# Gates loaded into the tiles of their results, two additions made by transfers, and sums of squares in two chains taken half a product later, in a hybrid short-convolution and Conformer block

## The chip, the cores and the metric

The kernel runs on one core of a Trainium2 chip, in one launch. The metric is the time on the device in microseconds (us) of one execution; the median of three runs is compared. The names of the engines are those of the profile: PE (TensorE, matmuls), DVE (VectorE), ACT (ScalarE), POOL (GpSimd) and SP (SyncE, which only starts transfers here). Each engine works through its own instructions in a fixed order and waits at an instruction whose inputs, or whose place to write, are not ready.

## The reference

One layer on 1024 rows of 1024 channels in f32: two mixers side by side, merged by sigmoid gates, and a feed-forward layer with SwiGLU behind them.

```python
h = rms_norm(x, norm_mix_g[l]) * (1.0 + sc1) + sh1
proj = jnp.einsum('bsd,de->bse', h, w_in[l])
b_s, c_s, v_s, v_c, gl_c, gate_br = jnp.split(proj, SPLITS[:-1], axis=-1)
y_a = b_s * causal_dwconv(c_s * v_s, conv_short_w[l])
y_a = jnp.einsum('bsc,cd->bsd', y_a, w_short_out[l])
u = v_c * jax.nn.sigmoid(gl_c)
u = causal_dwconv(u, conv_conf_w[l]) + conv_conf_b[l]
u = jax.nn.silu(layer_norm(u, conf_ln_g[l], conf_ln_b[l]))
y_b = jnp.einsum('bsc,cd->bsd', u, w_conf_out[l])
g_a, g_b = jnp.split(jax.nn.sigmoid(gate_br), 2, axis=-1)
mix = jnp.einsum('bsd,de->bse', g_a * y_a + g_b * y_b, w_o[l])
x = x + g1 * mix
h2 = rms_norm(x, norm_ffn_g[l]) * (1.0 + sc2) + sh2
a, bgate = jnp.split(jnp.einsum('bsd,df->bsf', h2, w_ffn_in[l]), 2, axis=-1)
x = x + g2 * jnp.einsum('bsf,fd->bsd', jax.nn.silu(a) * bgate, w_ffn_out[l])
return rms_norm(x, final_norm_g)
```

`sh1, sc1, g1, sh2, sc2, g2` are six vectors of 1024, `silu(c) @ w_ada + b_ada`.

## The kernel before

The activations are held transposed: a tile has 128 channels on its partitions, and the 1024 rows are two halves of 512, called h. Eight tiles j = 0..7 make up a tensor.

Every large product is cut into 2x2 blocks in Strassen-Winograd's way: seven products m ("1" to "7") in place of eight, for each of the two outputs (d = 0, 1, the two groups of four output tiles, which share their sums of operands). Each operand is carried as a high and a low part in fp32r, and three matmuls stand for one: weights' high by high (L553), high by low (L554), low by high (L556). One call of `product` does one (d, m): for p = 0 and 1 four such triples into one PSUM bank, so 24 matmuls, and hands each finished bank to an `evac` function. An argument `between` of `product` is called between p = 0 and p = 1.

The weights of a product come in by a transfer that SP starts (`raw`). Where a sum of blocks is wanted, POOL adds other blocks to it by transfers that accumulate (L368, L403). ACT casts the high part (`wh`, L254, 128x1024), DVE subtracts for the low part (`wl`, L255), two products ahead of their use. The same pair of engines splits the activations (`q4h` and `q4l`, `z2h` and `z2l`, `h20h` and `h20l` and so on).

A scheduler fixes each engine's order when the kernel is built, from costs and from the sizes of the pools of buffers; two pools matter here. `g_tile` gives one of 6 buffers of 128x512, for short-lived tiles: gates (`ga`, `gb`), squares (`sq`), residual inputs (`xr`), reciprocal roots. `s_tile` and `hl_tile` draw on a pool of 58 buffers, for results that live longer (`ma`, and the split operands). A tile's load can start only when the last reader of the buffer's former tile is done.

The stages that the change touches stand in this order:

- **The short branch's output product** (560 to 645 us of the profile). `ya_evac` takes the banks; `out` multiplies a finished block by its gate `ga` into the result `ma[j, h]` (L914 or L918). `gates_a`, called ahead of each product, starts the two loads of gates that the product's results will want: on ACT's queue for m = "2" and on SP's otherwise. Beside it DVE normalizes the other branch (`cv`, `mu`, squares `sq`, sums `suml` for the matmuls `var` at L733), and multiplies the modulation's weights (`ada`, L534).
- **The Conformer branch's output product** (645 to 745 us). `yb_evac` multiplies by the gates `gb` and adds the result to `ma`: either by DVE (L1463) or by a transfer of POOL's that accumulates (L1467). Which one is set by d, row and h. The operands `z1` to `z7` are split meanwhile.
- **The merged product** (745 to 795 us, `mix`, in the order "1267453" of m). `mix_evac` adds the bank to the residual tile `x1[j]`; `x1_done` stores the finished half, squares it on ACT and adds the square to `sums[h]`. For h = 0 DVE adds; for h = 1 the odd j are added by POOL's transfers through `onto` (L618) and the even ones by DVE (L1546). `norm_2_first` splits `sums[0]` into `sumh` and `suml` (L726, L727), sums them over the partitions by two matmuls (L733) and makes the reciprocal root `r2r`. `norm_2_rows` then scales half 0 of the rows k that it is given and splits them (`h2k`, L1622, L1628). `NORM_2_AT` and `NORM_2_ROWS` say at which products of d and m this happens.
- **The feed-forward input products** (from 795 us on), whose first product reads `h20` to `h23`; the sum of half 1 over the partitions is two matmuls (`ss`, L739) in the middle of the product (1, "1"), and its root is taken at L629 to L631.

Of the kernel before, what the change touches and what calls it, by code (L numbers as in the profile page):

```python
# [38 lines left out]
ALU = mybir.AluOpType  # L39
# [5 lines left out]
KC = D // P  # L45
# [44 lines left out]


NORM_2_AT = (1, "5")
NORM_2_ROWS = {(1, "5"): (0, 1, 2, 3), (0, "3"): (4, 5), (1, "3"): (6, 7)}

# [53 lines left out]
def block_kernel(ctx: ExitStack, tc: tile.TileContext, x0, xT, c, vecs, ada, w_first, w_plain, w_duals,  # L150
                 w_short, w_conf, w_o, w_fi, w_fo0, w_fo1, outT):
    nc = tc.nc
# [33 lines left out]
    def hl_tile(name, dt=F32R):  # L186
        return tp.tile([P, H], dt, tag="t", name=name)

    def s_tile(name, dt=F32):
        return hl_tile(name, dt)  # L190

    def g_tile(name):
        return gsp.tile([P, H], F32, tag="gs", name=name)
# [4 lines left out]
    halves = (slice(0, H), slice(H, T))  # L198
# [366 lines left out]
    def product(banks, m, t, evac=None, between=None, y_tile=ps2_tile, z_tile=ps_tile, onto="", by_k=False):  # L565


        w = next_w()
        b = {"1": "x", "6": "x", "7": "x", "4": "x", "2": "y", "5": "z", "3": "z"}[m]
        n = len(t)  # L570
        if by_k:
            for k in range(n):
                for p in range(2):
                    c0 = (p * n + k) * P
                    mm3([banks[b, p]], slice(c0, c0 + P), w, [t[k]], m not in onto and k == 0, k == n - 1, m in onto)
            for p in range(2):
                evac(p, m, banks[b, p])
            return
        for p in range(2):
            if (b, p) not in banks:  # L580
                banks[b, p] = {"x": ps_tile, "y": y_tile, "z": z_tile}[b](b)
            ps = banks[b, p]
            for k in range(n):
                c0 = (p * n + k) * P
                mm3([ps], slice(c0, c0 + P), w, [t[k]], m in "125" and m not in onto and k == 0, k == n - 1, m in "6734" + onto)
            if evac:
                evac(p, m, ps)
            if between and p == 0:
                between()
# [26 lines left out]
    def onto(a, b):  # L616

        return nc.gpsimd.dma_start(a, b, accum_op=ALU.add).ins  # L618
# [125 lines left out]
    gate_dram = {(b, j): dram.tile([P, T], F32, name=f"gate_{b}{j}") for b in "ab" for j in range(KC)}  # L744
# [637 lines left out]
    ma = {}  # L1382

    def ya_evac(d, banks):

        st = {}

        def out(i, row, h, op, ps):
            j = 4 * d + 2 * i + row
            ma[j, h] = s_tile(f"ma{j}{h}")  # L1390
            op(ma[j, h], ps, gas.pop((j, h)))
            ma["ins"] = plus.ins

        def evac(i, m, ps):
            if m == "1":
                if d == 1:
                    banks["y", i] = ps2_tile("y")
                nc.scalar.copy(banks["y", i], ps)
            elif m in "65":
                st[m, i] = s_tile("vz")  # L1400
                nc.scalar.copy(st[m, i], ps)
            elif m == "2":
                with tc.issue_after(split_w.lo):
                    out(i, 0, 0, times, ps)
            elif m == "7":
                z = ps2_tile("z")
                plus(z, ps, st["5", i])
                out(i, 1, 1, minus_times, z)
            elif m == "3":
                plus(ps, ps, st["6", i])  # L1410
                out(i, 0, 1, times, ps)
            else:
                out(i, 1, 0, minus_times, ps)
        return evac

    gas = {}

    def gates_a(d, m):
        row, h = {"2": (0, 0), "7": (1, 1), "3": (0, 1), "4": (1, 0)}.get(m, (0, None))
        for i in range(2 * (h is not None)):  # L1420
            j = 4 * d + 2 * i + row
            gas[j, h] = g_tile("ga")
            (nc.scalar if m == "2" else nc.sync).dma_start(gas[j, h], gate_dram["a", j][:, halves[h]])

    ya_banks = [{(bank, p): ring[(1 + n) % 3][p] for bank, n in (("x", 2 * d), ("y", 1), ("z", 1)) for p in range(2)}
                for d in range(2)]
# [21 lines left out]
    tm = {m: [None] * KH for m in PRODUCTS}  # L1448
# [5 lines left out]
    def yb_evac(d, banks):  # L1454

        st = {}

        def out(i, row, h, op, src):
            j = 4 * d + 2 * i + row
            g = gbs.pop((j, h))  # L1460
            op(g, src, g)
            if d or (row, h) == (1, 0):
                nc.vector.tensor_tensor(ma[j, h], ma[j, h], g, ALU.add)  # L1463
            if (row, h) == (1, 0):
                tm_split("12"[d], j % KH, ma[j, h])
            elif d == 0:
                nc.gpsimd.dma_start(ma[j, h], g, accum_op=ALU.add)  # L1467

        def evac(i, m, ps):
            if m == "1":  # L1470
                nc.scalar.copy(banks["y", i], ps)
            elif m in "65":
                st[m, i] = s_tile("vz")
                nc.scalar.copy(st[m, i], ps)
            elif m == "2":
                out(i, 0, 0, times, ps)
            elif m == "7":
                plus(st["5", i], ps, st["5", i])
                out(i, 1, 1, minus_times, st["5", i])
            elif m == "3":  # L1480
                plus(st["6", i], ps, st["6", i])
                out(i, 0, 1, times, st["6", i])
            else:
                out(i, 1, 0, minus_times, ps)
        return evac
# [41 lines left out]
    sums, xrs = {}, {}  # L1527
# [8 lines left out]
    def x1_done(j, h, sq, ins):  # L1536
        dst = x1[j][:, halves[h]]
        nc.gpsimd.dma_start(x1_dram[j][:, halves[h]], dst)
        mix.sq = nc.scalar.activation(sq, dst, AF.Square, scale=1.0 / 32.0).ins
        if h not in sums:  # L1540
            sums[h] = sq
        elif h and j % 2:
            mix.add = onto(sums[h], sq)
        elif h:
            with tc.issue_after(h2_of.lo) if h2_of.lo else ExitStack():
                mix.add = nc.vector.tensor_tensor(sums[h], sums[h], sq, ALU.add).ins  # L1546
        else:
            mix.add = nc.vector.tensor_tensor(sums[h], sums[h], sq, ALU.add).ins
        mix.half_0 = ins
# [22 lines left out]
    def mix():  # L1572
        banks = [{} for _ in range(2)]
        for p in range(2):
            banks[0]["x", p] = ring[0][p]
            banks[0]["y", p] = banks[0]["z", p] = ps2_tile("y")
            banks[1].update({("x", p): ring[1][p], ("y", p): ring[2][p], ("z", p): ring[2][p]})
        evacs = [mix_evac(d, b) for d, b in enumerate(banks)]
        b = {(r, c): [ma[4 * r + k, c] for k in range(KH)] for r in range(2) for c in range(2)}

        def m_6(k):
            nc.vector.tensor_tensor(b[0, 1][k], b[0, 0][k], b[0, 1][k], ALU.subtract)
            t2m[k] = hl_tile("t2m", F32)
            minus(t2m[k], b[0, 1][k], b[1, 1][k])
            for r in range(2):
                onto(b[r, 0][k], t2m[k])
            tm_split("6", k, t2m[k])

        def m_7(k):
            tm_split("7", k, b[0, 0][k], True)  # L1590

        def m_4(k):
            tm_split("4", k, b[1, 0][k], True)

        steps = {
            (0, "2"): each(m_6, 0, 1), (1, "2"): each(m_6, 2, 3), (0, "6"): each(m_7, *range(KH)),
            (1, "6"): each(m_4, *range(KH)), (0, "7"): lambda: [tm_split("5", k, b[0, 1][k]) for k in range(KH)],
            (0, "4"): lambda: [tm_split("3", k, b[1, 1][k]) for k in range(KH)],
        }
        for i, (d, m) in enumerate(MIX_ORDER):  # L1600
            for step in MIX_ORDER[i + 1 : i + 2]:
                xr_loads(*step)
            if i in MOD_MIX:
                late_modulation(split.ins, i + 1 in MOD_MIX, lambda: s2p.tile([P, T], F32, tag="x1", name="ada"))
            if i == MOD_MIX[-1]:
                for k in range(KC):
                    affine(aff2, k, 32, vec, V_GFFN)
            if (d, m) == NORM_2_AT:
                norm_2_first()
            product(banks[d], m, tm[m], evacs[d], onto="2")  # L1610
            if (d, m) in NORM_2_ROWS:
                norm_2_rows(NORM_2_ROWS[d, m])
            if (d, m) == MIX_ORDER[-1]:
                load_rsqrt(mix.sq)
            steps.get((d, m), lambda: None)()
# [22 lines left out]
    def norm_2_first():  # L1638

        ss, hl = ring[1][0], parts(sums[0])  # L1640
        load_rsqrt(parts.ins)
        with tc.issue_after(mm3.ins):
            parts_sum(ss, hl)
        r2_0.append(rstd_end(*rstd_start(ss, eps1, "r2")))
# [288 lines left out]
    for g in range(FINAL):  # L1933
        for d in range(2):
            banks = {}
# [116 lines left out]
    for d in range(2):  # L2052
        banks = {}
# [3 lines left out]
    for i in range(1, len(PIECES)):  # L2057
        banks = {}
# [83 lines left out]
```

## Time and profile before

| what | value |
|---|---|
| median of three runs | 1441.52 us (1439.53 to 1441.76) |
| the profiled execution | 1442.58 us, of which the span between the first and last instruction is 1440.7 us |
| mean granted TensorE clock | 0.997 |
| PE busy | 1422.8 us, 99% |
| DVE, ACT, POOL busy | 1200.3, 664.6 and 536.8 us |
| DMA | 294.18 MB in the span |

The profile gives for each engine what share of the span it was busy, and the trace behind it each instruction's start, its length and, in square brackets, how long its engine stood idle before it and what ended that. A matmul's own length (389 ns) is longer than the distance to the next (0.23 us), since matmuls overlap. A row such as "x81" beside a busy time counts the matmuls in a stretch, and shows lost time more sharply than the busy time does.

### The profile page before, as it was taken

How to read it: one execution, taken by the hardware profiler on the slowest of the kernel's cores; microseconds unless marked ns; L12 is line 12 of the kernel's file. 1: busy time of each engine (PE TensorE's matmuls, PEld its weight loads, DVE VectorE, ACT ScalarE, POOL GpSimd, SP SyncE). 2: the span in 40 equal slices, each digit the busy share in tenths (PEclk: the TensorE clock that was granted, in tenths of full speed). 3: DMA queues.
4: the chain of work that ended last, by engine and by line, in shares of the span. 5: the costliest groups of instructions: out<-in, count | busy, mean ns of one | idle time of the engine just before them, and what ended most of it. 6: DMA issues, size and time to landing. Idle time of an engine off the chain costs nothing.

```text
span 1440.7 us, 17806 instructions
## 1 busy us (share of the span) xinstructions
PE 1422.8 (99%) x6274; PEld 1165.2 (81%) x6274; DVE 1200.3 (83%) x1681; ACT 664.6 (46%) x980; POOL 536.8 (37%) x525
## 2 busy tenths in 40 slices
PE   9999999999999999999999999999999999999997
PEld 5888888888888888787887788888888888888887
DVE  8987998999899999899989887777777675866676
ACT  4873333333333447466554674444444443312235
POOL 0017887777668661012121211110110015563405
PEclk9999999999999999999999999999999999999999
DMA  9775654333337879776797576555553449996903
GB/s 369 270 239 162 182 187 144 103 117 103 132 128 222 215 226 339 222 229 159 234 269 242 155 213 204 194 182 174 177 180 136 143 138 346 392 379 198 345 1 117
DMA packets 103163, 294.18 MB, mean 204 GB/s; under 512 B 11633, under 2 KB 13681, under 8 KB 103074
## 3 DMA queue, kind: packets, MB, share of 16 engines
q1 hardware_dynamic: 50992, 160.45, 32.6%
q0 software_dynamic: 46896, 118.96, 29.7%
q10 hardware_dynamic: 5186, 13.64, 2.4%
q8 instruction: 49, 0.80, 0.2%
q14 instruction: 40, 0.33, 0.1%
HBM read 218.82 MB, written 84.41 MB: 210 GB/s over the span
## 4 chain that ended last, share of the span: by engine, by line
PE 77%; issue 7%; DVE 7%; POOL 3%; ACT 3%; DMA 3%; SPq 0%; POOLq 0%; ACTq 0%; DVEq 0%
PE bank L556 11%; PE bank L553 10%; PE bank L554 10%; PE x L554 8%; PE x L556 8%; PE x L553 8%; PE z L553 4%; PE z L556 4%; PE z L554 4%; PE y L553 2%; PE y L554 2%; PE y L556 2%; PE lead L549 1%; POOL wl L255 1%; DVE wl L255 1%
## 5 line engine op out<-in xcount | busy, mean ns | idle before, releaser
L254 ACT CAST wh<-raw 128x1024 fp32r<-128x1024 f32 (+2 forms) x256 | 265.1, 1037 | 368.2 <-PE bank L554 129.4
L255 DVE TENSOR_TENSOR wl<-raw,wh 128x1024 fp32r<-128x1024 f32 (+2 forms) x178 | 213.7, 1201 | 47.6 <-ACT wh L254 45.7
L255 POOL TENSOR_TENSOR wl<-raw,wh 128x1024 fp32r<-128x1024 f32 x78 | 193.5, 2489 | 84.0 <-ACT wh L254 84.0
L1212 DVE SCALAR_TENSOR_TENSOR c<-diff,vec,c 128x512 f32<-128x512 f32 x232 | 163.3, 747 | 1.4
L1775 POOL DMA_DIRECT2D hid<-stage x70 | 37.4, 534 | 314.6 <-DVE stage L610 313.3
L556 PE MATMUL bank<-th,wl 128*128 128x512 f32 x336 | 130.8, 389 | 0.1
L554 PE MATMUL bank<-tl,wh 128*128 128x512 f32 x336 | 130.7, 389 | 0.0
L553 PE MATMUL bank<-th,wh 128*128 128x512 f32 x336 | 130.7, 389 | 0.0
L556 PEld LDWEIGHTS bank<-th,wl 128*128 128x128 f32 x336 | 63.1, 188 | 13.5 <-POOL wl L255 0.5
L554 PEld LDWEIGHTS bank<-tl,wh 128*128 128x128 f32 x336 | 63.1, 188 | 13.2
L553 PEld LDWEIGHTS bank<-th,wh 128*128 128x128 f32 x336 | 63.1, 188 | 13.0
L553 PE MATMUL x<-th,wh 128*128 128x512 f32 x176 | 68.5, 389 | 0.0
L554 PE MATMUL x<-tl,wh 128*128 128x512 f32 x176 | 68.5, 389 | 0.0
L556 PE MATMUL x<-th,wl 128*128 128x512 f32 x176 | 68.4, 390 | 0.0
L1212 DVE SCALAR_TENSOR_TENSOR c<-u,wsum,c 128x512 f32<-128x512 f32 x96 | 66.8, 750 | 0.8
L609 ACT CAST stage<-g 128x512 fp32r<-128x512 f32 x60 | 37.2, 620 | 63.3 <-DMA hid<-stage 36.9
L610 DVE TENSOR_TENSOR stage<-g,stage 128x512 fp32r<-128x512 f32 x60 | 41.2, 689 | 28.2 <-ACT stage L609 28.2
L1799 POOL DMA_DIRECT2D th<-hid x77 | 41.3, 536 | 51.2 <-PE x L556 23.9
L1799 POOL DMA_DIRECT2D tl<-hid x77 | 41.2, 536 | 19.1 <-DMA tl<-hid 3.8
L553 PE MATMUL bank<-t2h,wh 128*128 128x512 f32 x112 | 43.6, 389 | 0.0
L554 PE MATMUL bank<-t2l,wh 128*128 128x512 f32 x112 | 43.6, 389 | 0.0
L556 PE MATMUL bank<-t2h,wl 128*128 128x512 f32 x112 | 43.6, 389 | 0.0
(793 smaller groups left out, 4118.8 us busy)
## 6 DMA issues: line engine op xcount, KB each, us to landing
hid<-stage POOLq DMA_DIRECT2D x70, 512.0 KB, 4.6
raw<-in_w_duals SPq DMA_DIRECT2D x65, 512.0 KB, 3.9
raw<-in_w_fi SPq DMA_DIRECT2D x43, 512.0 KB, 4.7
th<-hid POOLq DMA_DIRECT2D x77, 256.0 KB, 6.0
tl<-hid POOLq DMA_DIRECT2D x77, 256.0 KB, 6.0
ada<-in_ada SPq DMA_DIRECT2D x34, 512.0 KB, 5.4
raw<-in_w_fo SPq DMA_DIRECT2D x16, 512.0 KB, 6.4
raw<-in_ada SPq DMA_DIRECT2D x14, 512.0 KB, 3.6
```

Source lines behind the costliest of these rows:

```text
L254: hi = nc.scalar.copy(wh, raw)
L255: lo = lo_engine.tensor_tensor(wl, raw, f32(wh), ALU.subtract)
L549: mm3.ins = nc.tensor.matmul(ps, w[0][:, wsl], x, start=first, stop=last, skip_group_check=again).ins
L553: nc.tensor.matmul(ps, wh, xh, start=first, stop=False, skip_group_check=again)
L554: nc.tensor.matmul(ps, wh, xl, start=False, stop=False, skip_group_check=again)
L556: mm3.ins = nc.tensor.matmul(ps, wl, xh, start=False, stop=last, skip_group_check=again).ins
L609: t_split.act = nc.scalar.copy(hi, src).ins
L610: t_split.ins = nc.vector.tensor_tensor(lo, src, f32(hi), ALU.subtract).ins
L1212: tap.ins = nc.vector.scalar_tensor_tensor(out=out, in0=src[:, s : s + H], scalar=wt, in1=acc, op0=ALU.mult, op1=ALU.add).ins
L1775: nc.gpsimd.dma_start(hid_dram[key], s)
L1799: nc.gpsimd.dma_start(t, hid_dram[key][:, s])
```

## The change

There are five edits.

1. The gates `ga` are loaded straight into the tile of the result, `ma[j, h]`, and the multiplication is done in place. The load draws on the pool of 58 buffers instead of that of 6.
2. The block (row 0, h 0) of d = 1 is added to `ma` by a transfer, as most blocks of d = 0 are, instead of by DVE. These are `ma40` and `ma60`, two additions.
3. For half 1 the squares of j = 1, 3, 5 are summed by transfers as before (j = 1 is where that chain starts), but the square of j = 7 starts a chain of its own, to which DVE adds the squares of 0 and 2, then the first chain, then the squares of 4 and 6. One transfer less, one addition by DVE more. An instruction that kept the additions behind the last split is gone.
4. `norm_2_first` is called between the two halves of product (1, "5") instead of ahead of it.
5. Row 5 is normalized after product (1, "3") instead of after (0, "3").

```diff
-NORM_2_ROWS = {(1, "5"): (0, 1, 2, 3), (0, "3"): (4, 5), (1, "3"): (6, 7)}
+NORM_2_ROWS = {(1, "5"): (0, 1, 2, 3), (0, "3"): (4,), (1, "3"): (5, 6, 7)}
...
-            ma[j, h] = s_tile(f"ma{j}{h}")
-            op(ma[j, h], ps, gas.pop((j, h)))
+            op(ma[j, h], ps, ma[j, h])
...
-            gas[j, h] = g_tile("ga")
-            (nc.scalar if m == "2" else nc.sync).dma_start(gas[j, h], gate_dram["a", j][:, halves[h]])
+            ma[j, h] = s_tile(f"ma{j}{h}")
+            (nc.scalar if m == "2" else nc.sync).dma_start(ma[j, h], gate_dram["a", j][:, halves[h]])
...
-            if d or (row, h) == (1, 0):
+            by_dma = d == 0 and (row, h) != (1, 0) or (row, h) == (0, 0)
+            if not by_dma:
                 nc.vector.tensor_tensor(ma[j, h], ma[j, h], g, ALU.add)
             if (row, h) == (1, 0):
                 tm_split("12"[d], j % KH, ma[j, h])
-            elif d == 0:
+            elif by_dma:
                 nc.gpsimd.dma_start(ma[j, h], g, accum_op=ALU.add)
...
         elif h and j % 2:
-            mix.add = onto(sums[h], sq)
+            if j < KC - 1:
+                mix.add = onto(sums[h], sq)
+            else:
+                sums["odd"], sums[h] = sums[h], sq
         elif h:
-            with tc.issue_after(h2_of.lo) if h2_of.lo else ExitStack():
-                mix.add = nc.vector.tensor_tensor(sums[h], sums[h], sq, ALU.add).ins
+            mix.add = nc.vector.tensor_tensor(sums[h], sums[h], sq, ALU.add).ins
+            if j == 2:
+                nc.vector.tensor_tensor(sums[h], sums[h], sums.pop("odd"), ALU.add)
...
-            if (d, m) == NORM_2_AT:
-                norm_2_first()
-            product(banks[d], m, tm[m], evacs[d], onto="2")
+            product(banks[d], m, tm[m], evacs[d], norm_2_first if (d, m) == NORM_2_AT else None, onto="2")
```

The scheduler's order moves with these edits at more places than the diff shows. Three of them follow; the numbers behind a name tell buffers apart.

On DVE in the short branch's product, where `ma_4806` and `ma_4820` (now `ma_4784` and `ma_4786`) are the results `ma40` and `ma60`, and `q4l` is the low part of an operand. The last `wl` here is the low part of the weights of product (0, "7"):

```order
 L1145 TENSOR_TENSOR q4l<-q_4011,q4h 128x512
-L914 TENSOR_TENSOR ma_4806<-y,ga 128x512
-L914 TENSOR_TENSOR ma_4820<-y,ga 128x512
+L1265 TENSOR_TENSOR cv_4820<-cv_4820,mu_4655 128x512
+L1265 TENSOR_TENSOR cv_4820<-cv_4820,mu_4659 128x512
+L255 TENSOR_TENSOR wl<-raw,wh 128x1024
+L914 TENSOR_TENSOR ma_4784<-y,ma_4784 128x512
+L914 TENSOR_TENSOR ma_4786<-y,ma_4786 128x512
 L1271 TENSOR_TENSOR sq<-sq 128x512 x2
-L255 TENSOR_TENSOR wl<-raw,wh 128x1024
```

Before, `wl` stood behind the two products with the gates and two additions of squares; now it stands ahead of them.

On ACT at the same place, the loads of the gates for `ma40` and `ma60` (`gate_a_130` and `gate_a_132`), the casts `q4h` and the casts `wh` of the weights; before:

```order
L254 CAST wh<-raw 128x1024
L1267 ACTIVATE sq<-cv_4776 128x512 x2
L1423 DMA ga<-gate_a_130 128x512
L1143 CAST q4h<-q_4005 128x512
L1423 DMA ga<-gate_a_132 128x512
L1143 CAST q4h<-q_4007 128x512
L254 CAST wh<-raw 128x1024
```

and now:

```order
L254 CAST wh<-raw 128x1024
L1143 CAST q4h<-q_4009 128x512
L254 CAST wh<-raw 128x1024
L1143 CAST q4h<-q_4011 128x512
L1420 DMA ma_4784<-gate_a_130 128x512
L1420 DMA ma_4786<-gate_a_132 128x512
L1267 ACTIVATE sq<-cv_4820 128x512 x2
```

The first load stood ahead of all four casts `q4h` and the second ahead of three of them, both ahead of the second cast of weights; now they stand behind all of these.

On ACT at the start of the Conformer branch's output product, where `z2h` are the high parts of the operand of the products "2", and the copies take the banks of the products "1" out of PSUM; before:

```order
L597 CAST z2h<-cv_4915 128x512
L1351 ACTIVATE cv_4968<-cv_4968,vec 128x512
L1471 COPY bank<-bank 128x512 x2
L597 CAST z2h<-cv_4968 128x512
L254 CAST wh<-raw 128x1024
L1471 COPY y<-bank 128x512 x2
```

and now:

```order
L1469 COPY bank<-bank 128x512
L254 CAST wh<-raw 128x1024
L1469 COPY bank<-bank 128x512
L1351 ACTIVATE cv_4911<-cv_4911,vec 128x512
L1351 ACTIVATE cv_4962<-cv_4962,vec 128x512
L597 CAST z2h<-cv_4911 128x512
L1469 COPY y<-bank 128x512
L597 CAST z2h<-cv_4962 128x512
```

The first cast `z2h` was ahead of the two copies of the first bank, and is behind them; the second is behind a copy of the second bank as well.

On DVE in the merged product, the additions of the squares of half 1 (`sq`) between the rows `h23l` and `h25l`; `x` are the rows of the residual. Before:

```order
L1628 SCALAR_TENSOR_TENSOR h23l<-x_6367,mod,h23h 128x512
L1563 SCALAR_TENSOR_TENSOR x_6134<-y,mod,x_6134 128x512
L1546 TENSOR_TENSOR sq<-sq 128x512
L1622 SCALAR_TENSOR_TENSOR x_6179<-x_6179,aff_107,r2r 128x512
L1546 TENSOR_TENSOR sq<-sq 128x512
L1622 SCALAR_TENSOR_TENSOR x_6410<-x_6410,aff_107,r2r 128x512
L1628 SCALAR_TENSOR_TENSOR h24l<-x_6179,mod,h24h 128x512
L255 TENSOR_TENSOR wl<-raw,wh 128x1024
```

and now:

```order
L1628 SCALAR_TENSOR_TENSOR h23l<-x_6351,mod,h23h 128x512
L1546 TENSOR_TENSOR sq<-sq 128x512
L1622 SCALAR_TENSOR_TENSOR x_6163<-x_6163,aff_107,r2r 128x512
L1546 TENSOR_TENSOR sq<-sq 128x512
L255 TENSOR_TENSOR wl<-raw,wh 128x1024
L1548 TENSOR_TENSOR sq<-sq 128x512
L1628 SCALAR_TENSOR_TENSOR h24l<-x_6163,mod,h24h 128x512
```

The addition of the first chain (L1548) has come in, and the scaling of row 5 (`x_6410` before) has gone behind this piece.

On PE in the same product, the two matmuls that sum `sumh` and `suml` over the partitions go twelve matmuls further down, into the middle of the product (1, "5"); `mg5h` and `mg5l` are its operand:

```order
 L556 MATMUL y<-mg5h,wl 128x512
-L733 MATMUL bank<-sumh,ones_c 128x512
-L733 MATMUL bank<-suml,ones_c 128x512
 L553 MATMUL bank<-mg5h,wh 128x512
...
 L556 MATMUL bank<-mg5h,wl 128x512
+L733 MATMUL bank<-sumh,ones_c 128x512
+L733 MATMUL bank<-suml,ones_c 128x512
 L553 MATMUL bank<-mg5h,wh 128x512
```

They stand between the halves of that product now, and ahead of both before.

More of the change, by code (lines that the diff above doesn't have):

```diff
@@ L1414, in ya_evac @@
         return evac
-    gas = {}
     def gates_a(d, m):
```

## The prediction

> **What bounds the kernel now.** I read the page first, for the share of each engine:
>
> ```profile
> PE 1422.8 (99%) x6274; PEld 1165.2 (81%) x6274; DVE 1200.3 (83%) x1681; ACT 664.6 (46%) x980; POOL 536.8 (37%) x525
> ```
>
> TensorE is the bound, and of the span's 1440.7 us it lacks 17.9. The change can only win back slots that PE loses in the stages it touches. A table of stretches of 20 us shows where these are; its columns are PE, PEld, DVE, ACT and POOL with busy time and count, then the granted clock, the DMA share and GB/s:
>
> ```profile
> 580.00:600.00 20.00, 17.81 (x71) 13.97 (x70) 15.40 (x23) 8.29 (x14) 0.00 (x0) 0.91 0.80 245
> 600.00:620.00 20.00, 20.00 (x90) 16.53 (x89) 20.00 (x31) 9.21 (x13) 1.75 (x2) 1.00 0.79 211
> 660.00:680.00 20.00, 18.99 (x80) 14.15 (x79) 20.00 (x29) 10.27 (x16) 5.48 (x8) 1.00 0.69 169
> 760.00:780.00 20.00, 18.50 (x81) 14.78 (x80) 18.99 (x30) 8.56 (x13) 3.12 (x6) 1.00 0.80 266
> 800.00:820.00 20.00, 18.22 (x79) 14.43 (x78) 18.78 (x27) 16.63 (x28) 2.89 (x4) 1.00 0.39 131
> 820.00:840.00 20.00, 19.68 (x86) 15.67 (x85) 19.08 (x28) 15.12 (x26) 5.29 (x6) 1.00 0.90 187
> 840.00:860.00 20.00, 20.00 (x90) 16.53 (x90) 16.89 (x24) 13.85 (x21) 2.17 (x4) 1.00 0.63 211
> ```
>
> A full stretch holds 90 matmuls, 0.222 us each. The five stretches short of that lack 19, 10, 9, 11 and 4, which is 4.2, 2.2, 2.0, 2.4 and 0.9 us: 11.7 us is the most that the change can bring. The waits of PE between 560 and 880 us (total, times, longest) name what it waited for:
>
> ```profile
> PE bank L556 <- DVE wl L255: 2.2, 1, 2.2
> PE ss L739 <- DVE sq L1546: 1.8, 1, 1.8
> PE bank L733 <- ACT sumh L726: 1.3, 1, 1.3
> PE bank L554 <- DVE z6l L598: 0.4, 1, 0.4
> ```
>
> So there are four places: `wl` of (0, "7") at 590 us, the splits `z5`, `z6` at 660 to 680, the sums of norm 2 at 776, and the squares' sum at 803. At each the work is late on DVE, mostly for want of room.
>
> **Place one: the gates.** The timeline of PE shows the stall and what follows it, and that of DVE why:
>
> ```profile
> 589.36 0.40 PE L554 MATMUL bank<-q7l,wh 128*128 128x512 f32 x1
> 591.94 0.50 PE L556 MATMUL bank<-q7h,wl 128*128 128x512 f32 x1 [2.19 <-DVE wl L255]
> 593.10 0.63 PE L553 MATMUL bank<-q7h,wh 128*128 128x512 f32 x1
> 595.66 0.63 PE L553 MATMUL bank<-q7h,wh 128*128 128x512 f32 x1
> ...
> 577.75 0.33 ACTq L1423 DMA_DIRECT2D ga<-gate_a  x1
> ...
> 578.64 1.04 ACT L254 CAST wh<-raw 128x1024 fp32r<-128x1024 f32 x1
> ...
> 588.86 0.69 DVE L914 TENSOR_TENSOR ma<-y,ga 128x512 f32<-128x512 f32 x1 [4.60 <-PE bank L554]
> ...
> 590.67 1.22 DVE L255 TENSOR_TENSOR wl<-raw,wh 128x1024 fp32r<-128x1024 f32 x1
> ...
> DMA to landing us min/median/max: 4.1/4.6/11.0
> ```
>
> DVE stood 4.6 us before the second product with a gate. The profile names a matmul, but that was long done; the gate's load started at 577.75 and the last line, from the view of the tile `ga`, has a longest flight of 11.0 us, so it came in at about 588.8. Behind it in DVE's queue stood `wl`, whose input had been cast at 578.64. PE waited 2.19 us for it and ran the next eight matmuls at half speed, 0.43 us apart where 0.22 is usual (593.10 to 595.66 is six steps): 1.7 us more.
>
> With the new order `wl` runs ahead of the gates' products, at about 583.6, so this stall and the slow matmuls go: 3.9 us at 596. But ACT starts the load later, behind a cast of 1.04 us and two `q4h`, so the same DVE queue is free for the rest at 588.8 to 590.3, with one `wl` less to do (1.2 us): DVE is 1.2 us earlier to 0.4 us later than before, while PE is 3.9 us earlier. The row of 600 to 620 shows DVE busy all the time, so it cannot catch up. The last thing that PE wants of it in this stage is the sum of squares at 624:
>
> ```profile
> 615.68 0.33 SPq L1340 DMA_DIRECT2D ada<-in_ada  x1
> ...
> 621.72 1.28 DVE L534 CUSTOM_DVE_ANT_0 ada<-ada,cs,vec 128x1024 f32<-128x1024 f32 x1 [0.19 <-DMA ada<-in_ada]
> 622.93 0.69 DVE L727 TENSOR_TENSOR suml<-sq,sumh 128x512 fp32r<-128x512 f32 x1
> ...
> 624.50 0.40 PE L733 MATMUL var<-suml,ones_c 128*128 128x512 f32 x1
> ```
>
> `suml` ends at 623.62 and is used at 624.50, so 0.88 us can be kept if DVE keeps its time, 2.0 if DVE is 1.1 us earlier. An earlier DVE meets the load of `ada`, which landed at the last moment already and is started only when the one before has been used; and the new order has this matmul one place earlier. I take 0.8 us, between 0 and 2.0. The rest of the 3.9 comes back as new waits at 600 to 625. The SP queue has six gates' loads ahead of one load of weights now; at 0.33 us each these are 2 us at a moment when the weights' buffer is itself waiting for its `wl`, so I count nothing; if that cover is gone, it costs those 2 us.
>
> **Place two: two additions of the Conformer branch.** Rows of ACT and DVE:
>
> ```profile
> 649.61 1.08 ACT L1471 COPY y<-bank 128x512 f32<-128x512 f32 x2
> ...
> 650.61 0.39 PE L554 MATMUL bank<-z2l,wh 128*128 128x512 f32 x1
> ...
> 662.21 1.29 DVE L1463 TENSOR_TENSOR ma<-ma,gb 128x512 f32<-128x512 f32 x2
> ```
>
> The new order puts the second `z2h` behind a copy of `y`. That copy starts at 649.61 and takes 0.54; the cast, half as wide as `wh`, takes 0.5, and the split as long as `suml`, 0.7: `z2l` is ready at 651.4 and wanted at 650.61. That is a loss of 0.8 us (0, if ACT has free time to start the copies sooner, to 1.5, if both copies stand ahead), which uses up what place one kept.
>
> Of DVE's queue the two additions take 1.29 us, in a stretch where DVE is busy 20.00 of 20 us and PE lacks 2.2. The order also has the splits and `wl` ahead of other work there. With 1.3 us less, and the splits first, I take the whole 2.2 us; half of it if ACT's casts, which alternate with DVE's splits, hold PE. The additions by POOL are covered: `ma40` and `ma60` are read only about 60 us later. But POOL is in order, and the load of a gate behind them waits for such a transfer to land:
>
> ```profile
> 657.33 1.76 POOL L1467 DMA_DIRECT2D ma<-gb  x2 [0.80 <-DVE gb L914]
> 663.01 0.57 POOL L1495 DMA_DIRECT2D gb<-gate_b  x1 [3.92 <-DMA ma<-gb]
> ...
> 669.08 0.90 POOL L403 DMA_DIRECT2D raw<-in_w_conf  x1 [3.90 <-DVE wl L255]
> ...
> 683.80 0.39 PE L553 MATMUL bank<-z3h,wh 128*128 128x512 f32 x1
> ```
>
> 663.01 − 657.33 is 5.7 us, so the sum of weights that started at 669.08 starts some 2 us later. Its product begins at 683.80, 14.7 us after; with 2 us each for the later start and the earlier PE it still has over 10 us for transfer, cast and `wl`. Cost nothing.
>
> **Place three: the sums half a product later.** PE's timeline:
>
> ```profile
> 776.30 0.39 PE L556 MATMUL y<-mg5h,wl 128*128 128x512 f32 x1
> 777.96 0.50 PE L733 MATMUL bank<-sumh,ones_c 128*128 128x512 f32 x1 [1.28 <-ACT sumh L726]
> 778.69 0.50 PE L733 MATMUL bank<-suml,ones_c 128*128 128x512 f32 x1 [0.23 <-DVE suml L727]
> 779.03 0.40 PE L553 MATMUL bank<-mg5h,wh 128*128 128x512 f32 x1
> ```
>
> From 776.30 to 779.03 are 2.73 us for three steps of 0.23, so 2.0 us are lost. Twelve matmuls later the sums are wanted at 776.53 + 2.72 = 779.25, after `suml` was ready (at 778.69 at the latest, when PE used it). The stall goes, 2.0 us. The root and the rows `h20` to `h23` behind it come up to 0.7 us later, and PE reaches them 2 us sooner. Between the sums and their first use lie three products of 24 matmuls, 16 us, for one root, four scalings and eight splits of under 0.8 us each: cost nothing, and up to 2.7 us if DVE does other work first.
>
> **Place four: squares in two chains.**
>
> ```profile
> 803.32 0.39 PE L556 MATMUL x<-h23h,wl 128*128 128x512 f32 x1
> 805.49 1.12 PE L739 MATMUL ss<-sq,ones 128*128 128x512 f32 x2 [1.78 <-DVE sq L1546]
> ...
> 796.50 0.69 DVE L1546 TENSOR_TENSOR sq<-sq 128x512 f32<-128x512 f32 x1 [3.18 <-DMA sq<-sq]
> ...
> 804.75 0.68 DVE L1546 TENSOR_TENSOR sq<-sq 128x512 f32<-128x512 f32 x1
> ```
>
> The third transfer of squares goes, and with it DVE's wait of 3.18 us; one addition (0.6) comes. The last addition ends at 805.43 now. 3.18 − 0.6 is 2.6 us earlier, 802.8. PE, 2.0 us earlier by place three, wants it at 803.55 − 2.0 = 801.5, and so waits 1.3 in place of 1.9 (805.49 − 803.55). The gain at 806 is 2.0 + 0.6 = 2.6. DVE then has the scalings and splits to 840, 19.08 of 20 us busy, and is 2.6 us earlier at best, with the rest of the reordering 2 to 2.5: I keep 2.1 us of places three and four (1 to 3.5).
>
> **Sum.** 0.8 − 0.8 + 2.2 + 2.1 = 4.3 us. From 840 on every stretch is full, so it stays. The profiled execution, 1442.58 us, becomes 1438.3; it lies 1.06 us above the median shown, so the median becomes 1441.52 − 4.3 = 1437.2. The bounds together give 0 − 1.5 + 0.5 + 1 = 0 to 2.0 + 0 + 2.2 + 3.5 = 7.7 us. A measurement of this kernel can tell about 0.2%, 2.9 us, from no change.
>
> **The clock.** After the stall of 2.19 us the granted clock of the stretch is 0.91, and eight matmuls ran at half speed; after those of 1.28 and 1.78 us it is 1.00. The Trainium skill ("TensorE: Matmul & The Clock Gate", section "HAM oscillation — how this bites in real kernels") gives the rule that PE must not idle for more than about 3.4 us. By that rule a new wait of 2 us costs only itself; by this trace it can cost 1.7 us more, and the measurement decides. None of the new waits that I foresee is above 1.9 us, so the sum stands by either.
>
> **Rivals.**
>
> *All stalls go, 8 to 10 us, 1431.5 to 1433.5.* If the gates' load, issued without waiting for a buffer, lands at its median flight of 4.6 us (by 585), DVE is 4 us earlier from 590 on and keeps the 3.9; with 2.2, 2.0 and 1 the sum is 9.1: 1432.4. Against it: the load of `ma60` waited for no buffer for long before either, and flew 11 us. Chance 0.13.
>
> *Only norm 2 wins, 1 to 2.8 us, within 0.2%.* DVE's waits eat place one, and at 660 to 680 ACT's casts hold PE, so that the additions taken off DVE only lengthen its idle time. For it: PE waited there for ACT's `wh` too (0.2 us), and a reordering moves work on both engines. 1441.52 − 2.1 = 1439.4. Chance 0.28.
>
> *Slower: the gates come too late.* ACT starts the two loads about 2 us later, behind the casts. Each us by which the product of `ma60` starts after 590 delays DVE, which has no free time until 627, and the sum `suml` with it. From a start 1 us later than before (589.9) PE would be later at 624.5 than now; when the wait at `var` then passes 2.2 us, the half clock adds 1.7. A load 3 us later gives 3 − 0.9 + 1.7 = 3.8 us, less 0.8 to 2 of norm 2 and with ACT's 0.8 on top: 2 to 4 us slower, 1443.5 to 1445.5. Against it: the flight ends with the crowd of transfers at 588, so a later start shortens it. Chance 0.12.
>
> *My own forecast,* a gain of 2.9 to 8 us, has 0.47. Its own range is 1433.8 to 1438.6. To faster by over 0.2% go 0.47 + 0.13 = 0.60, to within 0.2% 0.28, to slower 0.12. The range that leaves out the upper part of the slower case and the lower of the best is 1432.5 to 1443.5.
>
> **What would show it.** Right: no wait for `wl` at 590 and a clock of 1.00 in that stretch, but new waits of PE for `wl` or `suml` at 600 to 627; 85 to 90 matmuls in the stretch that starts at 660; no wait for `sumh`; a wait of about 1.3 us at `ss`. Wrong: the product of `ma60` after 590.5, waits at `z2`, `z5` or `z6` as long as before, or a stretch with a clock below 1.00.

## The result, and the profile after

| | before | changed |
|---|---|---|
| median | 1442.76 us (1439.53 to 1449.54, 22 runs) | 1439.45 us (1437.01 to 1442.76, 22 runs) |
| profiled execution | 1442.58 us, span 1440.7 us | 1441.20 us, span 1439.1 us |

The ratio is 0.9973 with a 95% interval of 0.9964 to 0.9982: the change makes the kernel 0.27% faster, 3.9 us of the median before, where 4.3 were forecast. The two medians lie 3.3 us apart. The four places of the prediction do not add up to this in the way it said, though. First the stretches of the changed kernel (columns as before):

```profile
580.00:600.00 20.00, 20.00 (x90) 16.56 (x89) 17.02 (x25) 10.24 (x16) 0.75 (x1) 1.00 0.90 261
600.00:620.00 20.00, 19.02 (x83) 15.13 (x82) 20.00 (x31) 9.29 (x14) 1.75 (x2) 1.00 0.80 206
620.00:640.00 20.00, 19.75 (x87) 15.74 (x86) 17.52 (x28) 13.24 (x17) 3.13 (x5) 1.00 0.79 223
640.00:660.00 20.00, 17.66 (x70) 13.64 (x69) 17.32 (x26) 12.42 (x20) 2.35 (x3) 0.91 0.63 172
660.00:680.00 20.00, 20.00 (x90) 16.55 (x89) 20.00 (x30) 12.55 (x19) 8.36 (x12) 1.00 0.89 194
760.00:780.00 20.00, 20.00 (x90) 16.53 (x90) 19.68 (x32) 7.61 (x10) 2.71 (x5) 1.00 0.83 268
800.00:820.00 20.00, 19.78 (x86) 15.75 (x85) 19.89 (x29) 18.12 (x30) 4.32 (x6) 1.00 0.45 122
820.00:840.00 20.00, 19.52 (x85) 15.54 (x84) 19.25 (x29) 15.30 (x26) 3.85 (x5) 1.00 0.87 217
```

The stretches from 580, 660 and 760 are full now, and that from 800 nearly. A new hole has opened at 640 to 660: 70 matmuls and a clock of 0.91. PE's waits between 560 and 880 us name it:

```profile
PE bank L554 <- DVE z1l L598: 2.3, 1, 2.3
PE bank L556 <- DVE wl L255: 0.5, 1, 0.5
PE bank L553 <- ACT wh L254: 0.5, 1, 0.5
PE x L553 <- ACT t2h L609: 0.3, 1, 0.3
PE var L733 <- DVE suml L727: 0.3, 1, 0.3
PE ss L739 <- DVE sq L1546: 0.2, 1, 0.2
```

`z1l` is the low part of the first operand of the Conformer branch's output product. Its story is in the timelines of PE, DVE and SP; the last two rows are SP's in the kernel before:

```profile
643.58 0.79 PE L554 MATMUL bank<-z1l,wh 128*128 128x512 f32 x1 [2.34 <-DVE z1l L598]
644.17 0.63 PE L556 MATMUL bank<-z1h,wl 128*128 128x512 f32 x1
...
637.54 0.68 DVE L598 TENSOR_TENSOR z1l<-cv,z1h 128x512 fp32r<-128x512 f32 x1
641.04 0.69 DVE L918 SCALAR_TENSOR_TENSOR ma<-z,ma 128x512 f32<-128x512 f32 x1 [2.81 <-DMA ma<-gate_a]
641.64 0.68 DVE L1350 TENSOR_TENSOR cv<-cv,rl0r 128x512 f32<-128x512 f32 x1
642.24 0.68 DVE L918 SCALAR_TENSOR_TENSOR ma<-z,ma 128x512 f32<-128x512 f32 x1
642.84 0.68 DVE L598 TENSOR_TENSOR z1l<-cv,z1h 128x512 fp32r<-128x512 f32 x1
...
620.01 14.43 SPq L238 DMA_DIRECT2D raw<-in_w_conf  x4
634.54 1.88 SPq L1420 DMA_DIRECT2D ma<-gate_a  x4
...
619.26 5.90 SPq L238 DMA_DIRECT2D raw<-in_w_conf  x3
625.22 5.83 SPq L1423 DMA_DIRECT2D ga<-gate_a  x4
```

DVE stood 2.81 us before the product of `ma51` with its gate. That gate's load, the first of four at 634.54, stands in SP's queue behind four loads of weights; the last of these (634.12, the end of a group that spans 14.43 us) waits for a buffer that DVE's `wl` gives free at 634.09. Before the change three of those loads stood ahead of the gates, and the gate's load began at 625.22. So DVE waits, `z1l` behind it waits, and PE waits 2.34 us and runs at half speed afterwards. Edit 1 alone already moves the loads there (below); a likely reason is that they no longer compete for the six buffers, but no run shows why the scheduler chose that place.

To see what each stage costs, the start of the same matmul is compared in two profiles. The table gives its start in the first profile of before minus its start in another, in us, so a rise is a gain; the columns on the left are other profiles of the same two kernels, on the right the experiments below: edit 1 alone (gates), edit 2 (adds), edits 3 to 5 (norm), edit 3 (chains), edits 4 and 5 (later), the changed kernel without edit 1 (no-gates), and the changed kernel with some gates' loads earlier (early). Points are times in the first profile of before.

```
point  before2 changed changed2 changed3 | gates  adds  norm chains later no-gates early early2 early3
 560    -3.82   -2.20   -2.62   -1.31    | -2.61 -0.79 -1.43 -6.13 -1.09  -2.33  -2.12 -1.68 -1.42
 598    -0.33    2.12    1.70    3.01    |  1.72  1.50 -0.85 -3.67 -1.13  -0.03   2.21  2.64  2.91
 627    -1.80    0.01    0.52    2.97    |  1.71  0.15 -0.85 -4.61 -1.13  -0.67   2.21  2.58  1.94
 660    -1.80   -4.48   -4.47   -1.16    |  0.45  0.15 -0.87 -4.64 -1.15  -0.70   2.21  2.58  1.92
 700    -1.81   -1.88   -1.88    1.44    |  1.55  1.31 -0.88 -4.66 -1.21   0.50   3.34  3.73  3.05
 785    -0.93    0.15    0.15    3.47    |  2.34  1.27  1.16 -3.52  0.83   2.53   5.37  5.76  5.08
 842    -0.15    1.58    1.54    4.78    |  3.06  1.33  1.38 -0.95 -3.38   3.81   6.38  5.96  6.52
```

Up to 570 us all these kernels have the same instructions in the same order, yet PE stands up to 6.1 us apart at 560. So the difference of two spans (1440.7 − 1439.1 = 1.6) is no measure of the change; from 560 on the first profile of the changed kernel is 1.58 + 2.20 = 3.8 us faster. That is no measure of it either: by the same sum the second profile of the kernel before is 3.82 − 0.15 = 3.7 us faster than its first, without any edit, and the other two of the changed kernel 4.2 and 6.1. The gain of the whole stands on the timed runs; the profiles show which waits come and go.

### The profile page after: what moved, and what is told of

It reads as the page before. It is cut to its first block, busy times and chain, and to the rows that moved or that the text cites. A ratio compares the mean times of both kernels' runs of the same rounds, so it can differ in the third digit from the quotient of the medians.

```text
span 1439.1 us, 17793 instructions
## 1 busy us (share of the span) xinstructions
PE 1421.6 (99%) x6274; PEld 1165.3 (81%) x6274; DVE 1201.5 (83%) x1680; ACT 664.0 (46%) x980; POOL 538.4 (37%) x526
## 4 chain that ended last, share of the span: by engine, by line
PE 79%; DVE 12%; issue 3%; POOL 2%; DMA 2%; ACT 1%; POOLq 0%; ACTq 0%; DVEq 0%; SPq 0%
PE bank L554 10%; PE bank L556 10%; PE bank L553 10%; PE x L554 8%; PE x L556 8%; PE x L553 8%; PE z L556 4%; PE z L554 4%; PE z L553 4%; PE y L553 2%; PE y L556 2%; PE y L554 2%; DVE c L1212 1%; PE lead L549 1%; DVE wl L255 1%
```

## The experiments

**Each edit alone.** Three kernels: the gates (edit 1), the two additions (edit 2), and the squares, the sums and row 5 (edits 3 to 5), each put into the kernel before, in the hunks that the diff above shows.

> Edit 1 alone (gates into the results' tiles). Theory A, that the new wait for z1l at 643 us comes from this edit, through the loads of ma51 and ma71 that now stand behind a load of weights in SP's queue: no wait for wl at 590 (4 us won), 2 us of it given back between 600 and 627, a wait for z1l of some 2.3 us with eight matmuls at half speed near 645 (4 us lost); the waits at 776 and 803 as before. In all 0 to 2 us slower than before, ratio 1.000 to 1.0015. Theory B, that the wait for z1l comes from the other edits' reordering or from chance: no such wait, 2 us faster, ratio 0.9985.

Measured: 1441.77 us (12 runs), ratio 0.9995 (0.9982 to 1.0008). The wait for `wl` at 590 is gone, and DVE waits for the gate of `ma51` here too, but less:

```profile
637.55 0.69 DVE L918 SCALAR_TENSOR_TENSOR ma<-z,ma 128x512 f32<-128x512 f32 x1 [1.00 <-DMA ma<-gate_a]
```

PE waited 0.6 us for `z1l`, and the clock of 640 to 660 was 1.00. The wait comes from this edit (theory A on the cause), but its size was not 2.3 us here and nothing was given back before 627, 1.3 us from there to 660. The waits at 776 and 803 were 0.5 and 1.2 us, not 1.3 and 1.8 as before. In the profile the edit gained; in the times it can't be told from nothing.

> Edit 2 alone (two additions by transfers). Theory A, that DVE's free 1.2 us close the gaps at 660 to 680: 88 to 90 matmuls in that stretch against 80, some 2 us faster, ratio 0.9985. Theory B, that the gaps closed in the changed kernel only because PE came there 4 us later, behind its wait for z1l: with PE on time the stretch lacks 6 to 10 matmuls still, 0 to 0.8 us faster, ratio 0.9995 to 1.0.

Measured: 1441.81 us (12 runs), ratio 0.9995 (0.9984 to 1.0007). The stretch that before had 80 matmuls:

```profile
660.00:680.00 20.00, 19.72 (x84) 15.29 (x83) 20.00 (x29) 10.73 (x16) 7.23 (x10) 1.00 0.81 190
```

PE gains 1.31 − 0.15 = 1.2 us between 660 and 700, about as much as the two additions took of DVE, and PE was on time there. That is between the theories: half of the hole closes, 6 matmuls are still lacking, and the time can't be told from no change. The other 1.4 us that the changed kernel gains in this stretch (2.6 in the first profile, −4.48 to −1.88) come only in the profiles in which PE has lost over 4 us before; that DVE gets ahead meanwhile is the likely reason.

> Edits 3, 4 and 5 alone (two chains of squares, the sums half a product later, row 5 later). Theory A, that norm 2 gains by itself what it gains in the changed kernel: no wait for sumh, a wait for ss of 0.5 us or less, 3.8 us faster at 806, ratio 0.9974. Theory B, that part of it came from DVE's being ahead there through the other edits: the wait for ss is 1 us or more and the gain 2 to 2.6 us, ratio 0.9983.

Measured: 1440.49 us (11 runs), ratio 0.9986 (0.9977 to 0.9996). The wait for `sumh` is gone (2.0 us at 785), but PE waits 1.4 us for the squares:

```profile
PE ss L739 <- DVE sq L1548: 1.4, 1, 1.4
```

In all 2.3 us from 700 to 842, theory B's size. In the changed kernel the same edits bring 3.3 to 3.5 us; there the wait was 0.2 to 0.3 us.

**Norm 2 taken apart.** Edit 3 alone, and edits 4 and 5 alone.

> Edit 3 alone (squares of half 1 in two chains). Theory A (DVE's wait for the third transfer made ss late): the wait for sumh at 776 as before, 1.3 us, and the wait for ss 1.2 us or less in place of 1.8; 0.6 to 1.5 us faster, ratio 0.999 to 0.9996. Theory B (DVE is full there, and the addition that comes in takes what the wait gives): the wait for ss 1.6 to 2 us, ratio 1.000.

Measured: 1441.07 us (12 runs), ratio 0.9987 (0.9977 to 0.9998); no wait for `ss` appears at all, and 2.6 us are gained from 785 to 842. This is more than theory A expected. The list has no wait for `sumh` either, though this kernel takes that sum where it stood before: in the five profiles of kernels that do so (before twice, edits 1, 2 and 3 alone), this wait was 1.3, 0.4, 0.5, 1.3 and none.

> Edits 4 and 5 alone (sums half a product later, row 5 later). Theory A: the wait for sumh gone, 2.0 us won at 785, and half of it or more kept at 842, since only the squares' sum takes some back; 1 to 2 us faster, ratio 0.9986 to 0.9993. Theory B (DVE paces PE there): the wait for ss grows by the 2 us that PE is earlier, to 3.5 us or more with half speed behind it, and the kernel is as slow as before or slower, ratio 1.000 to 1.001.

Measured: 1446.04 us (12 runs), ratio 1.0018 (1.0004 to 1.0032), slower than before. The sums are no longer waited for (2.0 us at 785), but then 4.2 us are lost. DVE and PE:

```profile
799.83 0.69 DVE L1546 TENSOR_TENSOR sq<-sq 128x512 f32<-128x512 f32 x1 [4.40 <-DMA sq<-sq]
801.70 1.22 DVE L255 TENSOR_TENSOR wl<-raw,wh 128x1024 fp32r<-128x1024 f32 x1
...
802.98 0.50 PE L556 MATMUL x<-h20h,wl 128*128 128x512 f32 x1 [2.37 <-DVE wl L255]
804.87 0.63 PE L553 MATMUL x<-h23h,wh 128*128 128x512 f32 x1
807.49 2.08 PE L739 MATMUL ss<-sq,ones 128*128 128x512 f32 x2 [1.13 <-DVE sq L1546]
```

DVE waits 4.40 us for the third transfer of squares, which POOL issued 2.8 us later than before (794.77 against 792.00), and `wl`, whose input is there, stands behind the addition. PE waits 2.37 us for `wl`, at half speed afterwards, and 1.13 for `ss`. Neither theory named that place: theory B had the sign and the half speed, but saw the wait at `ss`. With the third transfer gone this loss does not appear; but no gain of the later sums shows in the times either, for edits 3 to 5 together (0.9986) measure what edit 3 does alone (0.9987).

**The gates' loads ahead of the weights.** The changed kernel with two of `gates_a`'s calls one product earlier:

```diff
+    gates_at = {(1, "5"): "7", (1, "7"): "3", (1, "3"): ""}
     for i, (d, m) in enumerate(ya_order):
-        gates_a(d, m)
+        for g in gates_at.get((d, m), m):
+            gates_a(d, g)
```

> The changed kernel with the gates' loads of products (1, 7) and (1, 3) called one product earlier, so that SP starts those of ma51 and ma71 ahead of a load of weights and of ada, and one load of weights fewer stands ahead of ma41 and ma61. Theory A, that the wait for z1l is these loads' place in SP's queue: no wait for z1l, clock 1.00 at 640 to 660, 4 us won there. If nothing else is late, 7 to 8 us faster than before, ratio 0.9948. Theory B, that DVE then lacks room for z5 and z6 at 660 to 680, since PE comes on time: 1 to 2.5 us are lost there again, and the ratio is 0.996 to 0.9965.

SP's timeline shows that the loads of `ma51` and `ma71` start at 612 now, and those of `ma41` and `ma61` behind three loads of weights. Below it are DVE's products of the first pair and two stretches:

```profile
612.14 0.90 SPq L1420 DMA_DIRECT2D ma<-gate_a  x2
615.36 0.33 SPq L1340 DMA_DIRECT2D ada<-in_ada  x1
617.75 5.61 SPq L238 DMA_DIRECT2D raw<-in_w_conf  x3
623.46 0.85 SPq L1420 DMA_DIRECT2D ma<-gate_a  x2
...
630.10 1.28 DVE L918 SCALAR_TENSOR_TENSOR ma<-z,ma 128x512 f32<-128x512 f32 x2
...
640.00:660.00 20.00, 20.00 (x89) 16.44 (x88) 19.40 (x29) 16.64 (x25) 4.94 (x6) 1.00 0.61 155
660.00:680.00 20.00, 19.73 (x85) 15.32 (x85) 19.04 (x29) 12.07 (x19) 5.51 (x8) 1.00 0.80 181
```

No wait for `z1l`, no lost clock: PE keeps from 598 to 660 all that it had won. With the loads the scheduler also moved the products: DVE does those of `ma51` and `ma71` at 630.10, ahead of all of its `z1l`, and no longer among them. At 660 to 700 PE gains 1.1 us and not 2.6, as theory B said of that stretch. 1436.09 us (5 runs), ratio 0.9962 (0.9950 to 0.9974), in theory B's range; from 560 on 8.5 us in the profile.

**Both kernels again, side by side.**

> The changed kernel a second time, beside the one with earlier loads. Theory A (the wait for z1l comes from the loads of ma51 and ma71 behind a load of weights in SP's queue): DVE waits for the gate again ahead of ma51, by 1 to 3 us as the load flies 4.5 to 6.5 us, and PE waits for z1l by 0.5 to 2.3 us, at half speed behind it if the wait is above 2 us; ratio to before 0.9965 to 0.998. Theory B (chance): no wait of DVE ahead of ma51. What both expect: where PE stands at 560 us differs from the first profile by up to 2 us, since the order up to there is the same in all these kernels.

Measured: 1437.33 us (6 runs), ratio 0.9959 (0.9943 to 0.9975), a little faster than expected. The wait is back, longer:

```profile
640.88 0.69 DVE L918 SCALAR_TENSOR_TENSOR ma<-z,ma 128x512 f32<-128x512 f32 x1 [3.15 <-DMA ma<-gate_a]
...
PE bank L554 <- DVE z1l L598: 2.7, 1, 2.7
```

> The kernel with the earlier loads a second time, beside the changed kernel on the same chip. Theory A: no wait for z1l, and a median 2 to 4 us below that of the changed kernel, ratio to before 0.995 to 0.996. Theory B: the two kernels' medians agree within 1 us.

Measured: 1437.47 us (6 runs), ratio 0.9961 (0.9946 to 0.9975); no wait for `z1l` again. The two medians agree, as theory B expected, although this profile is 4.4 us shorter in span (1434.8 against 1439.2).

> The changed kernel a third time, beside the one with earlier loads, for the times: in the two profiled executions PE waited 2.3 and 2.7 us for z1l and these took 1441.2 us, while five timed runs of the last comparison took 1435.8 to 1438.6. Theory A (the wait with its half clock comes in a part of the executions): some of the timed runs lie above 1439 us, and the profile shows the wait again. Theory B (only under the profiler): the timed runs lie between 1435 and 1439, the profiled one 3 us or more above their median.

Measured: 1439.52 us (12 runs, 1435.25 to 1441.48), ratio 0.9973 (0.9961 to 0.9985). The wait for `z1l` is there a third time, 1.8 us and with lost clock. The profiled execution took 1438.03 us, and seven of the other eleven runs lie above 1439: so it is not the profiler that makes a run slow (theory B falls). What those seven waited for is not recorded, and PE's place at 560 alone differs by microseconds.

> The kernel with the earlier loads a third time. Theory A: no run above 1439 us, median 1 to 3 us below the changed kernel's; no wait for z1l in the profile. Theory B: the median within 1 us of the changed kernel's, and again no wait for z1l in the profile.

Measured: 1436.55 us (6 runs), ratio 0.9957 (0.9940 to 0.9973), again no wait for `z1l`; one run, 1440.77, is above 1439, against theory A's word. Over all runs the kernel with earlier loads has a median of 1436.88 us (17 runs, one above 1439) and the changed kernel 1439.31 (40 runs, 21 above 1439), a difference of 2.4 us (0.4 to 3.6, resampled from these runs). But the two were run side by side only twice, and there their medians differ by −0.1 and 3.0 us; these runs alone (12 and 18) give 1.7 us (−0.3 to 3.4). The ratios to before are 0.9957 to 0.9962 with earlier loads and 0.9959 to 0.9973 without. So the wait is gone in every profile, but how much time that saves is not settled.

**The changed kernel without edit 1.**

> The changed kernel without edit 1 (gates in tiles of their own again). Theory A: the wait for wl at 590 of about 2 us is back with half speed behind it, no wait for z1l, and the adds and norm 2 gain what they gain alone, 1.2 and 2.3 us in the profile: ratio 0.997 to 0.998, about that of the changed kernel, since edit 1 gives at 590 what it takes at 643. Theory B, that edit 1 is worth 2 us or more to the whole: ratio 0.9985 to 0.9995.

Measured: 1440.12 us (12 runs), ratio 0.9980 (0.9969 to 0.9991), so theory A's size. There is no wait for `z1l`; the wait at 590 is back, but the clock held:

```profile
593.59 0.50 PE L556 MATMUL bank<-q7h,wl 128*128 128x512 f32 x1 [1.73 <-DVE wl L255]
...
580.00:600.00 20.00, 18.27 (x81) 14.82 (x80) 15.96 (x24) 10.29 (x17) 0.00 (x0) 1.00 0.79 234
```

From 700 to 842 norm 2 gains 3.3 us here, more than the 2.3 that edits 3 to 5 gain alone. In the times, the three groups of edits multiply to 0.9995 × 0.9995 × 0.9986 = 0.9976, close to the 0.9973 of the whole. Of the three only norm 2 is clear of no change by itself; it accounts for about half of the gain, and how the rest divides between the gates and the additions is open.

**A second profile of the kernel before.**

> The kernel before a second time, to see what one execution's profile differs by from another's. Expected by all theories: the waits at 590, 776 and 803 again (2.2, 1.3 and 1.8 us within 0.5), and PE at 560 us up to 2 us later than in the first profile, since its first profile had no wait for POOL's wl at 470 to 500 and the others had.

Measured: 1442.92 us (one run). The expectation was wrong on the waits: the second profile of the kernel before has much smaller ones.

```profile
PE bank L556 <- DVE wl L255: 1.1, 2, 0.5
PE ss L739 <- DVE sq L1546: 1.0, 1, 1.0
PE bank L733 <- ACT sumh L726: 0.4, 1, 0.4
```

At 560 PE stood 3.82 us later than in the first, of which 3.3 are two waits that the first did not have (2.1 for ACT's `sig`, 1.2 for POOL's `wl`).

## Why the prediction was right or wrong

The sign, the likeliest case and the size of the sum were right: 4.3 us forecast, 3.9 measured (3.3 by the two medians), inside the 2.9 to 8 us of its own forecast. The time itself was not: 1439.45 us lies above the forecast 1437.2 and the range to 1438.6, of which 1.2 us is the base, whose median is 1442.76 over 22 runs and was 1441.52 over three. Two of the signs that it had named for being wrong came: the product of `ma60` after 590.5 in the first profile, and a stretch with a clock of 0.91 in all three. Of its terms some did not hold.

- **Place one, the stall at 590.** Right that it goes, with its half speed: 4.3 us in each of the three profiles of the changed kernel (560 to 598). New waits for `wl` and `suml` followed as forecast, and one for `wh`, in the first profile; in the second only `suml` (0.5 us), in the third none. The term "0.8, between 0 and 2.0 kept" was too small: 2.2, 3.1 and 4.3 us were left at 627. What was kept went with the landing of `ma60`'s gate. Its load flew 10.1, 8.9 and 7.3 us in these three profiles, where the prediction had seen 11.0, and 6.6 with the gates alone, where 4.3 us were kept as well. The earlier the product of `ma60` ran, the more was left:

```profile
590.75 0.69 DVE L914 TENSOR_TENSOR ma<-y,ma 128x512 f32<-128x512 f32 x1 [2.50 <-DMA ma<-gate_a]
...
589.95 0.69 DVE L914 TENSOR_TENSOR ma<-y,ma 128x512 f32<-128x512 f32 x1 [0.43 <-DMA ma<-gate_a]
...
586.24 1.47 DVE L914 TENSOR_TENSOR ma<-y,ma 128x512 f32<-128x512 f32 x2 [1.05 <-DMA ma<-gate_a]
```

The last row holds the products of `ma40` and `ma60`, the second at 587.02. Why the flight differs was not tried; without edit 1 it was 10.2 to 11.0 us in six of seven profiles.
- **The step that failed** is the sentence on SP's queue, where I counted nothing. It looked at the first six gates' loads, and for these that held. The four loads behind them moved behind one load of weights more, and that cost 4.5, 5.0 and 4.1 us from 627 to 660, where I had 0.8 for ACT's `z2h` (no profile lists a wait for `z2h` or `z2l`). All four profiles with edit 1 and these loads late have the wait for `z1l`, none of the seven without edit 1 has it, and none of the three with earlier loads, which lost nothing there. I had named a new wait of over 2 us with half clock as the slower rival, by ACT's queue at 590; the mechanism came, at another load and 50 us later.
- **Place two.** The additions are worth 1.2 us (1.1 to 1.2 from 660 to 700 with the adds alone, without the gates and with earlier loads; but 1.1 also came with the gates alone, without edit 2, after a wait for `z1l` of 0.6 us and in another order, so that the additions are not the only way to it). The 2.2 us that I took came in the changed kernel only where it had lost more just before. My lower value, half, was the right one for the edit by itself. The lower bound of the sum took 0.5 for it where half of 2.2 is 1.1, so its lower end was 0.6 and not 0.
- **Place three**: 2.0 forecast, 2.03 measured in each of the three profiles, against the first profile of before. The second was 0.9 us faster than the first there without any edit.
- **Place four**: with place three 2.1 forecast, 3.3 to 3.5 measured from 700 to 842: mis-sized. For edits 3 to 5 alone the working fits, with 2.3 us and a wait for `ss` of 1.4 where 1.3 was forecast. In the changed kernel that wait was 0.2 to 0.3 us; with the earlier loads it varied from 0.2 to 1.5 and the gain from 2.2 to 3.5, so what set it is open.
- **The base.** Part of what I set out to win was that one execution's luck. In the seven profiles of kernels with the gates as before, the stretch from 560 to 598 cost 4.3, 0.8, 2.0, 3.7, 1.9, 4.4 and 2.0 us (4.3 less each one's own gain there, in the order of the table: before, before2, adds, norm, chains, later, no-gates). The second profile of before gains 0.9 us from 700 to 785 and 0.8 from 785 to 842 on the first, without any edit. That the sum came out near is in part luck: terms set too high and too low met, and the stalls it was worked out from were larger than in the second profile.

What stays open: why the wait for `z1l` was 2.3, 2.7 and 1.8 us in the changed kernel and 0.6 with the gates alone, with the same order on SP. DVE waited 2.81, 3.15 and 2.31 us for the gate in the former and 1.00 in the latter, because the load took 6.4, 6.8 and 5.9 us from issue to landing there and 4.6 here; what made it slower was not tried.

## What to carry to other kernels

A load that no longer waits for a buffer is not thereby earlier: where the scheduler fixes a queue's order, look for the last load that it now stands behind, for every load that moved and not only the first group. An in-order engine that waits for such a load holds back whatever stands behind it, even when that is ready. Here starting the load earlier removed the wait; the scheduler then moved the work too, so the two are not told apart. Two edits at one place should be priced together: the later sums lose 0.18% alone and nothing that can be measured once the third transfer is gone. And take a second profile before pricing a stall of 2 us: the stall of 2.2 us at 590 was at most 0.5 in the second profile of the same program.

## What was not expected of the hardware

The clock. From 20 us on, waits of 1.0 to 1.78 us that found PE at full speed were not followed by matmuls at half speed in these profiles, with one exception, and those of 2.19 us and more were; in between it came out both ways. Rows from the kernel with edits 3 to 5, the third profile of the changed kernel, and the second profile of before, and at the end the exception, from edits 4 and 5:

```profile
592.79 0.51 PE L556 MATMUL bank<-q7h,wl 128*128 128x512 f32 x1 [1.83 <-DVE wl L255]
...
640.12 0.50 PE L554 MATMUL bank<-z1l,wh 128*128 128x512 f32 x1 [1.82 <-DVE z1l L598]
641.48 0.63 PE L554 MATMUL bank<-z1l,wh 128*128 128x512 f32 x1
...
464.15 0.50 PE L553 MATMUL bank<-h41h,wh 128*128 128x512 f32 x1 [2.07 <-ACT sig L967]
464.49 0.40 PE L554 MATMUL bank<-h41l,wh 128*128 128x512 f32 x1
...
591.92 0.50 PE L553 MATMUL bank<-q7h,wh 128*128 128x512 f32 x1 [1.75 <-ACT vz L1401]
593.31 0.80 PE L556 MATMUL bank<-q7h,wl 128*128 128x512 f32 x1 [0.66 <-DVE wl L255]
593.90 0.63 PE L553 MATMUL bank<-q7h,wh 128*128 128x512 f32 x1
```

After the first two the clock of the stretch is 0.91, and matmuls 0.43 us apart begin about 1.4 us after the second; after the third it stays at 1.00. The exception is two waits of 1.75 and 0.66 us within 3.2 us, with matmuls 0.43 us apart behind the second and 0.91 in that stretch again. All lie below the 3.4 us of the Trainium skill's rule that the prediction weighed against the trace. The Trainium skill says on the same page ("TensorE: Matmul & The Clock Gate", section "What's actually happening") that the gate watches a free-running window; these runs agree in that a wait of about 2 us may or may not cost the clock. I had said that no new wait above 1.9 us was to be foreseen and that the sum stood by either rule; a wait of 1.82 us was enough.
